# Attention scores of a hybrid encoder block: the keys' low part multiplied over 128 rows instead of 64

## The chip, the cores and the metric

The kernel runs as one program on one core of a Trainium2 chip. The metric is the device time of an execution in microseconds. It is given as the median of the runs; single executions are shown with the profile, which was taken from one further execution.

## The reference

The reference is one layer of a bidirectional encoder, 1024 tokens of width 1024, in float32. A mixer with two branches (a Hyena long convolution and grouped-query attention) is followed by an expert-choice feed-forward layer with 16 experts. The part that matters here is the attention: 8 query heads of width 64, and 2 heads of keys and values, each shared by 4 query heads.

```python
q = (apply_axial_rope(rms_norm(q, q_gain), cos, sin) * (HEAD_DIM ** -0.5))
k = apply_axial_rope(rms_norm(k, k_gain), cos, sin)
...
def block(qblk):                       # 128 queries
    s = jnp.einsum('bkgqd,bksd->bkgqs', qblk, k)
    p = jax.nn.softmax(s, axis=-1)
    return jnp.einsum('bkgqs,bksd->bkgqd', p, v)
```

## The kernel before

**Two parts of each number.** TensorE's operands are in a shortened 32-bit float type. To keep the precision, the kernel splits an operand into a high part and the low rest, and adds up several products of parts in one PSUM bank. The helper `mm3` (lines 141 to 144) does this with three matmuls: high by high, high by low, low by high.

**Stages.** `mixer_head` computes the Hyena branch, the projections and the layouts of queries, keys and values. `attention` computes the scores, the softmax and the product with V, and fills in Hyena's output projection (`hyena_out`). `merge` and `project` combine the branches and add the residual. `experts` runs the feed-forward layer, for which most of the weights are loaded.

**Layout of queries and keys.** A head has only 64 channels, and a matmul can contract over 128 rows (partitions). The queries of a head, `QT[h]`, therefore hold both parts in one tile of 128 rows: for an even head the low rows are the high part and the upper rows the low part, for an odd head it is the other way round (lines 609 to 619). The keys are held in `KT[0][kv]` (high part) and `KT[1][kv]` (low part), each with the same 64 channels written twice, to the lower and the upper rows (lines 600 to 604). So one matmul of 128 rows with `KT[0]` gives (high + low part of the queries) times the high part of the keys. The second matmul adds the low part of the keys. Its rows `pr` are those of the queries' high part alone: 0 to 63 for an even head, 64 to 127 for an odd one.

**The order of the work in attention.** A unit is a head and two blocks of 128 queries, so there are 32 units, and each has 4 steps of 256 keys: 128 steps. In each step the loop at lines 867 to 878 traces: the transposes of the exponentials (`turned`, line 790) with the split of the result into `ph` on ScalarE (line 794) and `pl` on VectorE (line 795); one quarter of a later unit's scores (`scores`, lines 773 and 774); in two of three steps, a piece of Hyena's output projection (line 849); and the product of the previous step with V (`values`, lines 808 and 809). The scores run six quarters ahead of the steps. After two quarters, a block of queries has all its scores, and VectorE takes the maxima of the rows (line 779), ScalarE the exponentials (line 781). After the last step of every second unit `finish` scales the result (lines 814 to 827). The framework's scheduler fixes the order on each engine at build time, following this trace.

**Buffers.** The scores have two PSUM tiles of two banks (`pS`), the transposed exponentials two banks (`pM`), the results and the Hyena projection two (`pT`); `ph` and `pl` have two buffers each, the exponentials six. `QT` has two buffers, so the next head's queries are loaded while a head is worked on; the keys of the second head are loaded when the third query head starts. These loads are issued by GpSimd (lines 737 and 747), and those of the weights by SyncE.

**What follows attention.** The first weights of the experts are loaded when a certain step of the projection is done (line 963, kept as `late`).

Of the kernel before, what the change touches and what calls it, by code (L numbers as in the profile page):

```python
# [17 lines left out]
DRAM = bass.MemoryType.DRAM  # L18
# [33 lines left out]
def block(tc, xT, cols_d, rows_d, mlp_d, w4_d, dfc_d, idf_d, rope_d, wada_d, win_d, why_d, watt_d, wout_d, wr_d,  # L52
# [3 lines left out]
    mm = nc.tensor.matmul  # L56
# [44 lines left out]
    @contextmanager  # L101
    def lane(n):
        """work for the gaps of what is traced outside: a later place in the scheduler's order"""
        keep = tc.cur_priority
        tc.cur_priority = max(lanes.get(n, 0), 1000000 * n)
        yield
        lanes[n] = tc.cur_priority
        tc.cur_priority = keep

    @contextmanager  # L110
    def in_order():
        """each engine runs what is traced inside in the order of the trace"""
        traced = nc.cur_bb.bb.instructions
        first = len(traced)
        yield
        prev = {}
        for i in traced[first:]:
            if i.engine in (mybir.EngineType.PE, mybir.EngineType.Activation, mybir.EngineType.DVE):
                if i.engine in prev:
                    tc.add_manual_dep(i, prev[i.engine], mybir.DependencyInfo(  # L120
                        mybir.DependencyClass.NoSync, mybir.DependencyReason.DATA), reason="in_order")
                prev[i.engine] = i.name

    def wait(late, early):
        """holds an instruction back for its turn"""
        tc.add_manual_dep(late.ins, early.ins.name, mybir.DependencyInfo(
            mybir.DependencyClass.Sync, mybir.DependencyReason.DATA), reason="wait")
# [18 lines left out]
    def rsqrt(r, v, t):  # L146
        """r = v ** -0.5, the square root's table refined by a Newton step"""
        nc.scalar.activation(r, v, AF.Sqrt)
        nc.vector.reciprocal(r, r)
        nc.vector.tensor_mul(t, r, r)  # L150
        nc.vector.tensor_mul(t, t, v)
        nc.vector.tensor_scalar(t, t, -0.5, 1.5, op0=ALU.mult, op1=ALU.add)
        nc.vector.tensor_mul(r, r, t)

    def adaln(acc, w, k):
        """one step in k of silu(c) @ w_ada, by partitions"""
        if k == 0:
            nc.vector.tensor_scalar(acc, w, siluc[:, 0:1], None, op0=ALU.mult)
        else:
            nc.vector.scalar_tensor_tensor(acc, w, siluc[:, k:k + 1], acc, op0=ALU.mult, op1=ALU.add)  # L160
# [19 lines left out]
    def mixer_head():  # L180
# [16 lines left out]

        # ---- Hyena filters' hidden layers, x's norms, the first shift and scale, h^T
        mlp = f4([128, NMLP])
# [38 lines left out]
        def columns(row):  # L238
            """a row of 1024 as the columns of [128, 8]"""
            t = z4([1, 1024])  # L240
            for hf in range(2):
                nc.scalar.copy(t[:, hf * 512:hf * 512 + 512], row[hf])
            ps = pM([128, 8])
            for m in range(8):
                mm(ps[:, m:m + 1], t[:, m * 128:(m + 1) * 128], ones[0:1, 0:1], start=True, stop=True)
            return ps
# [124 lines left out]

        # ---- input projection
        def win_block(m, evac, n=0):
# [25 lines left out]

        # ---- long convolutions  # L400
        def split2(t):
# [119 lines left out]
        spectra(1)  # L521
        # ---- q, k and v: norms, rotary positions, layouts for the products
        for m in range(12, 18):
# [81 lines left out]
        for i in range(2):  # L605
            for h in range(2):
                nc.sync.dma_start(KT_s[i, h], K[i][h].bitcast(F32))
        # the upper rows are those of the even heads' high parts and of the odd heads' low parts
        for b_ in range(4):
# [97 lines left out]

        # ---- the branch gates, and between them the rest of adaLN's projection
        after, tc.cur_priority = tc.cur_priority, before
# [14 lines left out]
    def attention(right):  # L724
# [29 lines left out]
        def scores(u, Ps):  # L754
            """in four steps: the scores of two blocks of queries, the rows' maxima, the exponentials"""
            h, i = u
            kv = h // 4
            if i == 1 and h < 7:
                QTs[h + 1], load = query(h + 1)
                wait(load, exps[-1])  # L760
            if u == (2, 0):
                keys(1)
            QT = QTs[h]
            pr = slice(h % 2 * 64, h % 2 * 64 + 64)
            if i % 2 == 0:
                rss[h, i // 2] = w("rs", [128, 12], bufs=3)
            rs = rss[h, i // 2]
            for j in range(2):
                qs = slice((i * 2 + j) * 128, (i * 2 + j + 1) * 128)
                S = pS()  # L770
                for n in range(2):
                    ns = slice(n * 512, n * 512 + 512)
                    mm(S[:, n], QT[:, qs], KT[0][kv][:, ns], start=True, stop=False)
                    mm(S[:, n], QT[pr, qs], KT[1][kv][pr, ns], start=False, stop=True)
                    if n == 0:
                        yield
                Sf = S.rearrange("p n k -> p (n k)")
                c = (i % 2) * 2 + j
                nc.vector.tensor_reduce(rs[:, c:c + 1], Sf, axis=AX.X, op=ALU.max, negate=True)
                P = w("P", [128, 1024], bufs=6)  # L780
                exps.append(nc.scalar.activation(P, Sf, AF.Exp, bias=rs[:, c:c + 1], accum_out=rs[:, 4 + c:5 + c]))
                Ps.append(P)
                yield

        def turned(u, kk, Ps):
            """P^T's next two blocks of keys, split"""
            ps = pM()
            for n in range(2):
                for j in range(2):
                    nc.tensor.transpose(ps[:, n * 256 + j * 128:n * 256 + j * 128 + 128],  # L790
                                        Ps[j][:, (kk * 2 + n) * 128:(kk * 2 + n + 1) * 128], ident)
            ph = w("ph", [128, 512], F32R)
            pl = w("pl", [128, 512], F32R)
            nc.scalar.copy(ph, ps)  # L794
            nc.vector.tensor_sub(pl, ps, ph)  # L795
            return u, kk, ph, pl
# [31 lines left out]

        # ---- Hyena's output projection and gate, between the heads
        yh = yp.tile([128, 4, 1024], F32R, name="yh")  # L830
# [87 lines left out]
    def project(mTh, mTl, rc):  # L918
        """x1 = x + gt1 * (merged @ w_out), by columns d; its rows to DRAM; logits and sums of squares"""
        es = ExitStack()  # L920
# [22 lines left out]
        for m in range(8):  # L943
# [48 lines left out]
            for k in (0, 1) if m == 0 else (m + 1,) if m < 7 else ():  # L992
                adaln(acc, wload(wada_d[3, k]), k)
        # logits = r * (x1 @ (G2 w_router)) + sh2 @ w_router
        lT = wk.tile([NE, 1024], F32, name="lT", tag="sq", bufs=2)
# [27 lines left out]
    def choose(aff, r, rc, pT, w):  # L1023
        """the slot of each token in each expert's 128 (or -1), tokens in order; w and r as bf16 parts;
        the last instruction of TensorE before the choice"""
        es = ExitStack()
# [5 lines left out]

        # experts on partitions, in four chunks of tokens: each chunk's largest 128 in order
        ps = pT([128, 2, 128])
# [6 lines left out]
        for i in range(16):  # L1041
            V.max(m8[:, i], cur)
            nc.scalar.copy(up[0:64, 15 - i], m8[64:128, i])
            if i < 15:
                V.match_replace(wb[i % 2], m8[:, i], cur, -1.0)
                cur = wb[i % 2]
        # bf16 parts of the weights and of r, exact together
        wa = rc.tile([128, 8, NE, 3], BF16, name="wa")
# [11 lines left out]
        nc.gpsimd.tensor_copy(ra[:, :, 1], slots[:, 0:8])  # L1060
        # the largest 128 of two lists: of one's i-th and the other's i-th from the end, the larger;
        # the result falls, then rises; it is sorted, one of two chunks with its sign turned
        ab = [w("hl", [128, 512])[0:64, 0:128] for i in range(2)]
# [3 lines left out]
        a, b = ab  # L1067
# [9 lines left out]
        V.tensor_reduce(T, b[0:32], axis=AX.X, op=ALU.min)  # L1077
        # the 128th largest, to each token's partition; those above it, and of those equal to it the first
        Tb = pT([128, NE])
# [27 lines left out]
    def experts(aff, r, rc, raws, n_raw, late):  # L1107
# [16 lines left out]
        def load(src, n):  # L1124
            """1 MB in n rows a partition; not before the projection's end, nor ahead of the first tokens' gather"""
            raw = raws.tile([128, 4, 512], F32, name="raw", tag="raw", bufs=n_raw)
# [21 lines left out]
        def halves(src, e):  # L1148
            cuts = 4 if e == NE - 1 else 1
            o = []  # L1150
            for i in range(2):
                raw = load(src[:, None, i * 2048:i * 2048 + 2048], 1)
                h = w("eh", [128, 4, 512], F32R, 5)
                l = w("el", [128, 4, 512], F32R, 5)
                # the first of them while VectorE chooses
                eng = nc.gpsimd if len(loaded) <= 9 else nc.vector
# [115 lines left out]
        for e in range(NE):  # L1272
            for f in range(4):
# [4 lines left out]
                last = (e, f)  # L1278
                # the next expert's tokens, each step behind work that covers the wait for it
                if e + 1 < NE:  # L1280
# [160 lines left out]
```

## Time and profile before

The median of three runs is 2301.83 us (2300.32 to 2301.86). The profiled execution has a span of 2299.0 us from the first to the last instruction.

| from the profile | value |
|---|---|
| runs, median | 2301.83 us |
| profiled execution, span | 2299.0 us |
| TensorE matmuls, busy | 2188.9 us, 95% |
| TensorE weight loads, busy | 1687.6 us, 73% |
| VectorE, busy | 1909.1 us, 83% |
| ScalarE, busy | 1307.3 us, 57% |
| mean granted TensorE clock | 0.981 |
| DMA, mean rate over the span | 256 GB/s |

A busy share is the time with an instruction at work on the engine, divided by the span; matmuls are pipelined, so that one starts while the one ahead is still counted. PE stands for TensorE's matmuls, PEld for its weight loads, DVE for VectorE, ACT for ScalarE, POOL for GpSimd, SP for SyncE. In a group such as `pS<-KT,QT 64*128 64x512`, the result stands ahead of the arrow, then the operands; `64*128` is the rows and columns of the array that are used, and `64x512` the moving operand, rows by columns.

### The profile page before, as it was taken

To read this page: it belongs to the slowest core of one execution; us is meant where nothing else is said; L and a number is where in the kernel's file an instruction comes from. 1 tells how busy PE (TensorE), PEld (TensorE's weight loads), DVE (VectorE), ACT (ScalarE), POOL (GpSimd) and SP (SyncE) were. 2 spreads that over 40 slices of the span, in tenths; PEclk is the share of its full clock that TensorE was granted. 3 is DMA by queue.
4 is the path that set the end of the run, shared out by engine and by line. 5 is a ranking of instruction groups with operands and counts; after the bars stand their busy time and mean duration, and the time that the engine had idled before them with its cause. 6 is when DMAs were issued, how large, how long until landed. Compare 5 with 4: busy or idle time off the path is not lost. (4 is left out here: it accounts for less than half of the span.)

```text
span 2299.0 us, 26847 instructions
## 1 busy us (share of the span) xinstructions
PE 2188.9 (95%) x10076; PEld 1687.6 (73%) x10076; DVE 1909.1 (83%) x2149; ACT 1307.3 (57%) x1424; POOL 126.2 (5%) x130
## 2 busy tenths in 40 slices
PE   5799999999999999999699999999999999999997
PEld 1487887878677777766477777777777777777776
DVE  6888897998887777743798998988989889898886
ACT  5554454242376555212477676767677676776775
POOL 1011000010000000000400010000000000000000
PEclk8899999999999999999799999999999999999999
DMA  7155755554532112756599999999999999999994
GB/s 276 29 146 195 282 201 162 176 166 138 165 119 79 55 62 70 247 196 248 207 360 361 365 343 360 351 365 373 353 373 369 363 374 353 369 371 364 371 336 152
DMA packets 138134, 588.87 MB, mean 256 GB/s; under 512 B 13714, under 2 KB 34450, under 8 KB 88724
## 3 DMA queue, kind: packets, MB, share of 16 engines
q1 hardware_dynamic: 122308, 546.25, 63.5%
q0 software_dynamic: 15696, 40.90, 6.9%
q8 instruction: 79, 1.29, 0.2%
q14 instruction: 51, 0.42, 0.1%
HBM read 530.48 MB, written 56.62 MB: 255 GB/s over the span
## 5 line engine op out<-in xcount | busy, mean ns | idle before, releaser
L1161 DVE TENSOR_TENSOR el<-raw,eh 128x2048 fp32r<-128x2048 f32 (+1 forms) x451 | 861.5, 1946 | 66.6 <-ACT eh L1160 66.4
L1160 ACT CAST eh<-raw 128x2048 fp32r<-128x2048 f32 (+1 forms) x456 | 719.0, 1635 | 62.0 <-PE py L144 31.6
L142 PE MATMUL pM<-eh,xh 128*128 128x512 f32 x1024 | 406.9, 397 | 8.1 <-ACT eh L1160 6.3
L143 PE MATMUL pM<-el,xh 128*128 128x512 f32 x1024 | 406.4, 397 | 8.5 <-DVE el L1161 8.3
L144 PE MATMUL pM<-eh,xl 128*128 128x512 f32 x1024 | 402.1, 393 | 0.0
L143 PEld LDWEIGHTS pM<-el,xh 128*128 128x128 f32 x1024 | 192.9, 188 | 61.8 <-DVE el L1161 25.1
L142 PEld LDWEIGHTS pM<-eh,xh 128*128 128x128 f32 x1024 | 192.7, 188 | 50.7 <-ACT eh L1160 9.1
L142 PE MATMUL pM<-hT,wh 128*128 128x512 f32 x544 | 217.6, 400 | 4.7 <-ACT wh L137 3.7
L144 PEld LDWEIGHTS pM<-eh,xl 128*128 128x128 f32 x1024 | 192.9, 188 | 37.7
L144 PE MATMUL pM<-hT,wl 128*128 128x512 f32 x544 | 216.2, 398 | 0.6 <-DVE wl L138 0.6
L143 PE MATMUL pM<-hT,wh 128*128 128x512 f32 x544 | 216.5, 398 | 0.0
L143 PE MATMUL py<-el,hh 128*128 128x512 f32 x512 | 207.1, 404 | 1.3 <-DVE el L1161 1.3
L142 PE MATMUL py<-eh,hh 128*128 128x512 f32 x512 | 203.7, 398 | 1.9 <-ACT hh L1236 1.9
L144 PE MATMUL py<-eh,hl 128*128 128x512 f32 x512 | 202.3, 395 | 0.1
L137 ACT CAST wh<-wr 128x1024 fp32r<-128x1024 f32 (+1 forms) x60 | 56.0, 934 | 166.7 <-PE pM L143 82.4
L142 PEld LDWEIGHTS pM<-hT,wh 128*128 128x128 f32 x544 | 102.8, 189 | 29.1 <-ACT wh L137 4.2
L794 ACT CAST ph<-pM 128x512 fp32r<-128x512 f32 x128 | 74.9, 585 | 84.6 <-PE pM L790 79.4
L144 PEld LDWEIGHTS pM<-hT,wl 128*128 128x128 f32 x544 | 102.6, 189 | 25.0 <-DVE wl L138 1.3
L143 PEld LDWEIGHTS pM<-hT,wh 128*128 128x128 f32 x544 | 102.8, 189 | 23.6
L142 PEld LDWEIGHTS py<-eh,hh 128*128 128x128 f32 x512 | 96.1, 188 | 28.5 <-ACT hh L1236 6.3
L795 DVE TENSOR_TENSOR pl<-pM,ph 128x512 fp32r<-128x512 f32 x128 | 87.2, 687 | 34.2 <-ACT ph L794 33.6
L143 PEld LDWEIGHTS py<-el,hh 128*128 128x128 f32 x512 | 96.2, 188 | 24.6 <-DVE el L1161 3.1
(367 smaller groups left out, 3468.6 us busy)
## 6 DMA issues: line engine op xcount, KB each, us to landing
raw<-in_wg_dram SPq DMA_DIRECT2D x128, 1024.0 KB, 7.1
raw<-in_wu_dram SPq DMA_DIRECT2D x128, 1024.0 KB, 7.1
raw<-in_wd_dram SPq DMA_DIRECT2D x128, 1024.0 KB, 7.8
wr<-in_win_dram SPq DMA_DIRECT2D x34, 512.0 KB, 3.6
dc<-in_dfc_dram POOLq DMA_DIRECT2D x48, 256.0 KB, 3.0
wr<-in_wada_dram SPq DMA_DIRECT2D x24, 512.0 KB, 3.7
st<-in_wada_dram SPq DMA_DIRECT2D x16, 512.0 KB, 10.2
H<-H_s SPq DMA_DIRECT2D x16, 512.0 KB, 4.2
```

The lines of the kernel that those rows point to most:

```text
L137: nc.scalar.copy(h, raw)
L142: mm(o, a[0], b[0], start=start, stop=False)
L143: mm(o, a[0], b[1], start=False, stop=False)
L144: mm(o, a[1], b[0], start=False, stop=stop)
L794: nc.scalar.copy(ph, ps)
L795: nc.vector.tensor_sub(pl, ps, ph)
L1160: nc.scalar.copy(h[:, ks], raw[:, ks])
L1161: eng.tensor_sub(l[:, ks], raw[:, ks], h[:, ks])
```

## The change

The second product of the scores runs over all 128 rows of the queries and of the low part of the keys, and no longer over the 64 rows `pr`. The result gains the product of the queries' low part with the keys' low part. The lines of the helper variable are gone; comments are blanked elsewhere in the file, which is not shown.

```diff
             QT = QTs[h]
-            pr = slice(h % 2 * 64, h % 2 * 64 + 64)
             if i % 2 == 0:
                 rss[h, i // 2] = w("rs", [128, 12], bufs=3)
...
                     mm(S[:, n], QT[:, qs], KT[0][kv][:, ns], start=True, stop=False)
-                    mm(S[:, n], QT[pr, qs], KT[1][kv][pr, ns], start=False, stop=True)
+                    mm(S[:, n], QT[:, qs], KT[1][kv][:, ns], start=False, stop=True)
```

## Prediction

> **What bounds the kernel now.** I read the page's busy shares first, then the windows of the stretch in which the changed instructions run, then the groups of that stretch, its waits, and last the instructions in order of time. The chain that ended last was of no use: it holds only the final DMA and some issue time.
>
> ```profile
> span 2299.0 us, 26847 instructions
> PE 2188.9 (95%) x10076; PEld 1687.6 (73%) x10076; DVE 1909.1 (83%) x2149; ACT 1307.3 (57%) x1424; POOL 126.2 (5%) x130
> ```
>
> TensorE is busy for 95% of the whole span, but a busy TensorE may still be waiting inside an instruction, so the stretch has to be looked at by itself. The second product of the scores runs there:
>
> ```profile
> L774 PE MATMUL pS<-KT,QT x128: 490/498/504, 624.4 to 896.4; 64*128 64x512 f32 x128
> ```
>
> It starts 128 times, first at 624.4 us and last at 896.4 us. The windows around that (busy us and instructions of each engine, granted clock, DMA share, GB/s):
>
> ```profile
> 600.00:634.00 34.00, 28.90 (x122) 20.38 (x120) 26.57 (x32) 17.22 (x24) 4.75 (x9) 0.95 0.65 210
> 634.00:910.00 276.00, 275.97 (x1532) 205.57 (x1531) 209.35 (x286) 169.34 (x298) 4.99 (x10) 1.00 0.23 76
> 910.00:1010.00 100.00, 96.36 (x413) 71.10 (x413) 69.94 (x96) 23.11 (x35) 0.92 (x2) 1.00 0.66 219
> 1060.00:2299.00 1239.00, 1181.51 (x5427) 933.33 (x5426) 1072.89 (x1031) 833.48 (x720) 75.62 (x41) 0.98 0.91 341
> ...
> 640.00:660.00 20.00, 20.00 (x110) 14.37 (x109) 16.77 (x24) 15.15 (x30) 0.00 (x0) 1.00 0.35 117
> 800.00:820.00 20.00, 20.00 (x116) 15.09 (x115) 13.81 (x19) 11.20 (x20) 0.53 (x1) 1.00 0.22 79
> ```
>
> From 634 to 910 us, the attention proper, TensorE has no gap at all (275.97 of 276 us), VectorE is busy 209.35 us (76%), ScalarE 169.34 us (61%), and DMA has little to do (0.23). So TensorE's own stream sets the pace there. The last two rows are the window of 20 us in which VectorE is fullest, and the emptiest, of the 13 between 640 and 900 us.
>
> What TensorE does in that stretch, and beside what (groups from 634 to 911 us: busy us, mean ns of one, idle time just before them):
>
> ```profile
> L774 PE MATMUL pS<-KT,QT 64*128 64x512 f32 x123 | 61.0, 496 | 0.0
> L773 PE MATMUL pS<-KT,QT 128*128 128x512 f32 x122 | 54.7, 448 | 0.0
> L849 PE MATMUL pT<-yl,wh 128*128 128x512 f32 x64 | 25.6, 400 | 0.0
> L774 PEld LDWEIGHTS pS<-KT,QT 64*128 64x128 f32 x123 | 22.5, 183 | 28.9 <-issue 28.2
> L849 PEld LDWEIGHTS pT<-yh,wl 128*128 128x128 f32 x64 | 12.0, 188 | 11.3 <-issue 11.2
> L808 PEld LDWEIGHTS pT<-ph,Vhl 128*128 128x128 f32 x256 | 48.4, 189 | 12.0 <-issue 7.8 <-ACT ph L794 0.7 <-DVE ot L821 0.3
> ```
>
> A matmul of 64 rows takes longer (496 ns) than one of 128 rows and the same 512 columns in the same stretch (400 ns). And the weight loads of line 774 stand idle 28.2 us for "issue": they wait for nothing that a semaphore tells of. Durations overlap, so what counts is the time from one start to the next. TensorE's instructions in order of time (start, duration):
>
> ```profile
> 842.77 0.39 PE L849 MATMUL pT<-yh,wh 128*128 128x512 f32 x1
> 843.00 0.39 PE L849 MATMUL pT<-yl,wh 128*128 128x512 f32 x1
> 843.23 0.28 PE L808 MATMUL pT<-ph,Vhl 128*128 128x256 f32 x1
> ...
> 845.32 0.50 PE L849 MATMUL pT<-yh,wl 128*128 128x512 f32 x1
> 845.66 0.39 PE L773 MATMUL pS<-KT,QT 128*128 128x512 f32 x1
> 845.98 0.50 PE L774 MATMUL pS<-KT,QT 64*128 64x512 f32 x1
> 846.41 0.39 PE L808 MATMUL pT<-ph,Vhl 128*128 128x256 f32 x1
> 846.64 0.28 PE L809 MATMUL pT<-pl,Vhl 128*128 128x256 f32 x1
> 846.76 0.28 PE L808 MATMUL pT<-ph,Vhl 128*128 128x256 f32 x1
> ```
>
> In an undisturbed run a matmul of 512 columns is followed by the next after 0.23 us (842.77, 843.00, 843.23), one of 256 columns after 0.12 us (846.64, 846.76). Around a line 774 it is otherwise: 0.32 us from the first product to it, 0.43 us from it to the next, and the matmul behind it, of 256 columns, holds the next back for 0.23 us (846.41 to 846.64). The weight loads of the same moments say why:
>
> ```profile
> 843.00 0.19 PEld L808 LDWEIGHTS pT<-ph,Vhl 128*128 128x128 f32 x1
> 843.23 0.19 PEld L809 LDWEIGHTS pT<-pl,Vhl 128*128 128x128 f32 x1
> ...
> 845.98 0.18 PEld L774 LDWEIGHTS pS<-KT,QT 64*128 64x128 f32 x1 [0.36 <-issue]
> 846.41 0.19 PEld L808 LDWEIGHTS pT<-ph,Vhl 128*128 128x128 f32 x1 [0.25 <-DVE pl L795]
> 846.52 0.19 PEld L809 LDWEIGHTS pT<-pl,Vhl 128*128 128x128 f32 x1
> ```
>
> Between instructions of 128 rows a weight load starts together with the matmul ahead of its own (the load for 843.23 at 843.00) and is hidden. At line 774 it starts only with its own matmul (845.98), and so does the next full load (846.41): going from 128 rows to 64 and back, TensorE empties twice.
>
> On the 0.25 us of the last but one row the view names VectorE; the same gap follows line 774 where it names only issue, so I take it for the same thing.
>
> [...]
>
> **The change, part by part.** Nothing is added: the 128 second products keep their count, their 512 columns and their place; no DMA, no wait and no buffer is touched, since both halves of the low keys are loaded already. What changes is the form, from 64 to 128 rows, with three effects on TensorE for each instance:
>
> - the first product goes back to 0.23 us from 0.32: 0.09 us;
> - the second goes from 0.43 to 0.23: 0.20 us;
> - the one behind loses its exposed load: 0.23 to 0.12 us, or 0.34 to 0.23 where it has 512 columns (845.32 to 845.66): 0.11 us.
>
> Together 0.40 us. The price of a full-row second product is read off line 849, whose three matmuls accumulate in one bank in the same form; no row here shows two full loads of the very same queries in a row, which I put at no extra cost, because the load is 0.19 us and the matmul ahead gives it 0.23. In the attention proper 123 instances (of 128) stand: 123 x 0.40 = 49.2 us, and 5 stand before 634 us, where TensorE is busy 28.90 of 34 us and waits for others: between 0 and 2.0 us, taken as 0.
>
> Not all of it reaches the end. TensorE would then need 276 - 49.2 = 226.8 us, beside VectorE's 209.35 (92% of that). What is late next are the steps of P transposed: transposes on TensorE, the copy ph on ScalarE, the difference pl on VectorE, then the product with V. The waits from 634 to 911 us (total us, times, longest):
>
> ```profile
> ACT ph L794 <- PE pM L790: 79.4, 91, 2.6
> DVE pl L795 <- ACT ph L794: 33.6, 53, 1.3
> DVE rs L779 <- PE pS L774: 17.8, 22, 1.7
> DVE ot L821 <- ACT ot L820: 9.9, 10, 1.5
> DVE oT L827 <- ACT oT L825: 1.8, 3, 0.8
> PEld pT L809 <- DVE pl L795: 1.0, 4, 0.3
> ```
>
> TensorE waits for VectorE hardly at all today (1.0 us for pl). Behind a late pl queue the row maxima of the next scores (1.2 us each on VectorE), and for those the exponentials. Both ends of the loss: at best no stall, a gain of 49.2 (51.2 with the five early ones). At worst VectorE's waits for ScalarE all stay as they are, 33.6 + 9.9 + 1.8 = 45.3 us, and VectorE sets the stage at 209.35 + 45.3 = 254.7 us, a gain of 21.3. I expect those waits to shrink, because ScalarE itself waits for TensorE's transposes (79.4 us), which come sooner. For how dense TensorE stays with VectorE nearly full, the nearest row is the experts' stage: 1181.51 of 1239 us, 95%, with VectorE at 87%. So 226.8 / 0.95 = 238.7 us, a gain of 276 - 238.7 = 37.3 us.
>
> The stages behind move up rigidly: the merge, the projection and the experts start on results of attention, and the first expert weights wait for a step of the projection (line 963), not for the clock. DMA, at 0.91 in the experts' stage, gets no more to do and no less time. The sum: 2299.0 - 37.3 = 2261.7 us of span. The runs' median is 2301.83, 2.8 us above this span, so 2264.5 us, given as 2264.
>
> **The rivals.** *VectorE takes over as the bound.* Gain 21.3 us, 2280.5 us. For it: in the window at 640 us VectorE is busy 16.77 of 20 us, while TensorE there would need 20 - 0.40 x 123 x 20/276 = 16.4 us. Against it: that is the fullest of 13 windows, the emptiest has 13.81.
>
> *Everything passes through.* Gain 51.2 us, 2250.6 us. For it: buffers of two between the engines, and the 1.0 us that TensorE waits for pl today. Against it: VectorE would have to run at 92% with an order made for another pace.
>
> *Nothing changes.* This is so if the low keys' weight load stays exposed at 128 rows as well, and the drain belongs to the change of product rather than to the row form. [...] It would give 2301.8 us. [...]
>
> *Slower, through the clock.* With TensorE faster than its suppliers, gaps of some us appear at the heads' ends, and the granted clock falls behind each. The stretch before 634 us shows it: idle for 3.0 us (first row below), it then ran at 0.42 us from start to start instead of 0.23 (623.11 to 623.54), and its window has a clock of 0.95.
>
> ```profile
> 620.38 0.50 PEld L773 LDWEIGHTS pS<-KT,QT 128*128 128x128 f32 x2 [3.00 <-issue]
> 623.11 0.61 PE L144 MATMUL pT<-Zh,dc 128*128 128x512 f32 x1
> 623.54 0.42 PE L142 MATMUL pT<-Zh,dc 128*128 128x512 f32 x1
> ```
>
> One such event costs 3.0 us and 5% of 34 us, 4.7 us together. It takes eight of them, one in each head, to eat 37.3 us; two in each head, 75 us, would end at 2264.5 + 75 = 2339.5 us. Against it: the longest wait of any of these chains today is 2.6 us, and it is ScalarE's.
>
> **How the numbers follow.** The forecast, a gain between the two bounds with some stalls, gets 0.62 and gives the predicted 2264 us; its own range is 2255 to 2276. VectorE as the bound gets 0.18, everything passing 0.13, nothing 0.04, slower 0.03. The range takes in the first three, 0.93 in all, from 2250 to 2281 us; less would cut off one of the two bounds. I widen the lower end by a microsecond and the upper by two for the spread of the runs (2300.32 to 2301.86). A change under 0.2%, 4.6 us, can't be told from none. Faster: 0.62 + 0.18 + 0.13 = 0.93; same 0.04; slower 0.03.
>
> **What would show it.** In the changed profile the second product has the form 128*128, a mean near 400 ns, and no "issue" before its weight loads; the idle "issue" in front of lines 849 and 808 is gone with it. From start to start there should be 0.23 us before and after it. The stretch from the first scores to the last P transposed shrinks from 276 to some 239 us, with VectorE's busy time unchanged at 209 us and new, short waits of TensorE for pl and ph. The windows behind keep their lengths. The prediction is wrong in size if VectorE's idle time does not shrink with TensorE's, wrong in kind if a weight load of the second product still starts only with its matmul, or if the instructions come in another order than before.

## The result and the profile after

The changed kernel takes 2261.11 us (median of four runs, 2256.31 to 2262.78) against 2301.61 us of the kernel before on the same chip: a ratio of 0.9826 with a 95% interval from 0.9813 to 0.9840. It is faster by 40.5 us; the prediction had said 2264 us. The profiled execution has a span of 2259.4 us, 39.6 us less than that of before, and itself took 2261.17 us.

Where the 39.6 us lie is seen with the span cut at three events: the first and the last start of a product with V by `pl`, and the first cast of the experts' weights. The windows from the first of them to the end of the span, first of the kernel before and then of the changed one (busy us and instructions of PE, PEld, DVE, ACT, POOL; clock; DMA share; GB/s):

```profile
637.30:910.00 272.70, 272.67 (x1517) 203.61 (x1517) 206.74 (x283) 167.96 (x296) 4.46 (x9) 1.00 0.23 75
910.00:1090.70 180.70, 172.72 (x745) 125.64 (x745) 97.50 (x141) 38.89 (x65) 2.21 (x6) 0.97 0.64 222
1090.70:2299.00 1208.30, 1155.15 (x5305) 913.56 (x5303) 1064.26 (x1008) 824.06 (x701) 74.34 (x37) 0.98 0.92 345
```

```profile
637.40:870.80 233.40, 232.06 (x1516) 202.41 (x1517) 203.26 (x283) 167.41 (x296) 4.46 (x9) 1.00 0.27 88
870.80:1052.60 181.80, 172.81 (x745) 125.30 (x744) 97.53 (x141) 38.77 (x65) 2.21 (x6) 0.97 0.63 221
1052.60:2259.40 1206.80, 1153.04 (x5305) 912.32 (x5303) 1064.32 (x1008) 824.01 (x701) 74.34 (x37) 0.99 0.92 345
```

The first product with V starts at the same moment (637.3 and 637.4 us). The stage between the products, which I call the V window below, falls from 272.7 to 233.4 us: 39.3 of the 39.6 us. The two later stretches move up and keep their lengths within 1.5 us. VectorE and ScalarE run the same instructions as before and are busy 3.5 and 0.6 us less. The order of the instructions is the same on every engine.

The groups of the changed kernel from 634 to 871 us (the second product is line 773 now, the first 772, the Hyena projection 848, the products with V 807 and 808):

```profile
L772 PE MATMUL pS<-KT,QT 128*128 128x512 f32 x124 | 54.8, 442 | 1.0 <-ACT P L780 1.0
L773 PE MATMUL pS<-KT,QT 128*128 128x512 f32 x124 | 50.2, 404 | 0.0
L773 PEld LDWEIGHTS pS<-KT,QT 128*128 128x128 f32 x123 | 23.5, 191 | 0.5
L848 PEld LDWEIGHTS pT<-yh,wl 128*128 128x128 f32 x64 | 12.1, 189 | 1.6
L807 PEld LDWEIGHTS pT<-ph,Vhl 128*128 128x128 f32 x256 | 48.3, 189 | 8.3 <-DVE ot L820 2.1 <-ACT ph L793 1.4
```

The second product has 128 rows and a mean of 404 ns instead of 496, and the 28.2 us of "issue" ahead of its weight loads are gone; so are the 11.2 and 7.8 us of "issue" ahead of the two other groups. TensorE's instructions in order of time, and the weight loads under them:

```profile
814.32 0.39 PE L773 MATMUL pS<-KT,QT 128*128 128x512 f32 x1
814.55 0.40 PE L848 MATMUL pT<-yh,wl 128*128 128x512 f32 x1
814.78 0.40 PE L772 MATMUL pS<-KT,QT 128*128 128x512 f32 x1
815.01 0.39 PE L773 MATMUL pS<-KT,QT 128*128 128x512 f32 x1
815.35 0.39 PE L807 MATMUL pT<-ph,Vhl 128*128 128x256 f32 x1
```

```profile
814.55 0.19 PEld L772 LDWEIGHTS pS<-KT,QT 128*128 128x128 f32 x1
814.78 0.19 PEld L773 LDWEIGHTS pS<-KT,QT 128*128 128x128 f32 x1
815.35 0.19 PEld L807 LDWEIGHTS pT<-ph,Vhl 128*128 128x128 f32 x1 [0.38 <-DVE ot L820]
```

Four starts in a row are 0.23 us apart, where it was 0.32 and 0.43 us around a second product. Directly behind a group of transposes, where 56 of the 120 first products of the V window stand, the distance was 0.41 us and is 0.32, so 0.09 us are saved there too. The second product's weight load (814.78) starts under the first product. The last rows show what has come in its place: the product with V now waits for VectorE (`ot`). The waits from 634 to 871 us (total us, times, longest):

```profile
ACT ph L793 <- PE pM L789: 43.4, 68, 1.6
DVE pl L794 <- ACT ph L793: 14.4, 29, 1.2
DVE ot L820 <- ACT ot L819: 6.2, 10, 1.3
PEld pT L808 <- DVE pl L794: 4.4, 13, 0.7
PEld pM L789 <- DVE pl L794: 2.2, 6, 0.6
DVE oT L826 <- ACT oT L824: 0.9, 2, 0.5
```

### The profile page after: what moved, and what is told of

It reads as the page before. It is cut to its first block, busy times and chain, and to the rows that moved or that the text cites. A ratio compares the mean times of both kernels' runs of the same rounds, so it can differ in the third digit from the quotient of the medians.

```text
span 2259.4 us, 26847 instructions
## 1 busy us (share of the span) xinstructions
PE 2144.2 (95%) x10076; PEld 1684.7 (75%) x10076; DVE 1905.5 (84%) x2149; ACT 1306.7 (58%) x1424; POOL 126.3 (6%) x130
## 5 line engine op out<-in xcount | busy, mean ns | idle before, releaser
L144 PEld LDWEIGHTS py<-eh,hl 128*128 128x128 f32 x512 | 96.3, 188 | 21.2 <-DVE hl L1236 0.4
L1235 ACT CAST hh<-pT 128x512 fp32r<-128x512 f32 x64 | 37.3, 583 | 116.0 <-PE pT L1232 116.0
```

Source lines behind the costliest of these rows:

```text
L144: mm(o, a[1], b[0], start=False, stop=stop)
L1235: nc.scalar.copy(hh, pt)
```

## The experiments

The theory to test was that each change of form, from 128 rows to 64 and back, costs TensorE 0.40 us, and that a part of the saving is lost because VectorE becomes nearly full. This price is called a drain below. In the trace of the kernel before it stands as two weight loads that start only with their own matmuls, each 0.07 us before the matmul ahead is counted as over (the load at 845.98 with that one over at 845.66 + 0.39 = 846.05, the load at 846.41 with 845.98 + 0.50 = 846.48). The first four kernels ran with the kernel before at 2300.91 us, the next four at 2300.55 us, the last four at 2299.45 us.

**64 rows again, but in pairs.** Both first products of a block of queries come ahead of both second ones, which have 64 rows as in the kernel before.

```diff
-                for n in range(2):
-                    ns = slice(n * 512, n * 512 + 512)
-                    mm(S[:, n], QT[:, qs], KT[0][kv][:, ns], start=True, stop=False)
-                    mm(S[:, n], QT[:, qs], KT[1][kv][:, ns], start=False, stop=True)
-                    if n == 0:
+                pr = slice(h % 2 * 64, h % 2 * 64 + 64)
+                for i_ in range(2):
+                    r = pr if i_ else slice(0, 128)
+                    for n in range(2):
+                        ns = slice(n * 512, n * 512 + 512)
+                        mm(S[:, n], QT[r, qs], KT[i_][kv][r, ns], start=i_ == 0, stop=i_ == 1)
+                    if i_ == 0:
                         yield
```

> Undoes the row form, but halves the number of changes of form: the second products have 64 rows again, and both of a block of queries run one after the other, behind both first products (64 pairs instead of 128 single ones). Theory (the price is the draining of TensorE at a change of form, 0.40 us each time in and out): 64 x 0.40 = 25.6 us less than in the kernel before, some 2276 to 2280 us, and the second of a pair starts 0.23 us after the first. [...]

Measured: 2280.7 us, ratio 0.9909 (0.9892 to 0.9925), 20.2 us less than before. That is 0.7 us above the theory's range, and 7.4 us below the 2288.1 us that a saving at the neighbours alone would have given, 64 x (0.09 + 0.11) = 12.8 us. The scheduler left 54 of the 64 pairs together and pulled the others apart, so 54 drains are spared, 51 of them in the V window: 51 x 0.40 = 20.4 us. The V window falls from 272.7 to 253.2 us, 19.5 us. A pair in the trace: TensorE first, with the pair as one row (x2), then the pair's second product by itself, then the loads:

```profile
826.27 0.73 PE L775 MATMUL pS<-KT,QT 64*128 64x512 f32 x2
826.93 0.38 PE L809 MATMUL pT<-ph,Vhl 128*128 128x256 f32 x1
827.16 0.28 PE L810 MATMUL pT<-pl,Vhl 128*128 128x256 f32 x1
```

```profile
826.61 0.39 PE L775 MATMUL pS<-KT,QT 64*128 64x512 f32 x1
```

```profile
826.27 0.29 PEld L775 LDWEIGHTS pS<-KT,QT 64*128 64x128 f32 x2 [0.17 <-issue]
826.93 0.19 PEld L809 LDWEIGHTS pT<-ph,Vhl 128*128 128x128 f32 x1 [0.37 <-issue]
```

Two products of 64 rows take 0.66 us up to the next instruction. This sum is the theory's (0.43 + 0.23) and not that of two lone ones (0.43 + 0.43 = 0.86): the second one adds what a full one costs. How the sum is divided the theory did not have right: the second product starts 0.34 us after the first, and the next instruction 0.32 us after that. Both loads are over within 0.29 us of the first start, and a lone 64-row matmul is counted for 0.50 us (496 ns in the mean before), so the second load ran under the first 64-row matmul. The 64-row form is not dear in itself; the change of form is: TensorE's loads stand idle for 0.17 and 0.37 us at the two ends of the pair, and the view shows no gap between its two loads, which are in the same 64 rows.

**The control: pairs with 128 rows.** The same order, with all rows in both products.

```diff
-                for n in range(2):
-                    ns = slice(n * 512, n * 512 + 512)
-                    mm(S[:, n], QT[:, qs], KT[0][kv][:, ns], start=True, stop=False)
-                    mm(S[:, n], QT[:, qs], KT[1][kv][:, ns], start=False, stop=True)
-                    if n == 0:
+                for i_ in range(2):
+                    for n in range(2):
+                        ns = slice(n * 512, n * 512 + 512)
+                        mm(S[:, n], QT[:, qs], KT[i_][kv][:, ns], start=i_ == 0, stop=i_ == 1)
+                    if i_ == 0:
                         yield
```

> Control for the run with 64-row pairs: the same pairing of first and second products, with 128 rows. Theory: the order by itself is worth nothing, 2261 us as the changed kernel, within 3 us. Rival: the pairing itself changes the stalls (later or earlier maxima); then this run moves away from 2261 us and the run with 64-row pairs has to be read against it.

Measured: 2258.57 us, ratio 0.9816 (0.9799 to 0.9832); V window 234.4 us against 233.4. The pairing by itself is worth nothing in this stage, and the interval holds the changed kernel's ratio.

**Half of the change.** 64 rows for the first 512 keys, 128 for the last.

```diff
+                pr = slice(h % 2 * 64, h % 2 * 64 + 64)
                 for n in range(2):
                     ns = slice(n * 512, n * 512 + 512)
+                    r = slice(0, 128) if n else pr
                     mm(S[:, n], QT[:, qs], KT[0][kv][:, ns], start=True, stop=False)
-                    mm(S[:, n], QT[:, qs], KT[1][kv][:, ns], start=False, stop=True)
+                    mm(S[:, n], QT[r, qs], KT[1][kv][r, ns], start=False, stop=True)
```

> Half of the change: the second product has 64 rows for the first 512 keys and 128 rows for the last 512. Theory (0.40 us for each 64-row product, and stalls of TensorE come only when VectorE gets nearly full): TensorE's need falls by 64 x 0.40 = 25.6 us while VectorE stays under 84% of the stage, so nearly all of it reaches the end: 2276 to 2278 us. Rival (each us saved loses the same fifth to the coupling with ScalarE and VectorE, as 51.2 became 40.5): 25.6 x 0.79 = 20.2 us, 2281 us.

Measured: 2278.31 us, 22.6 us less than before; V window 251.6 us, 21.1 us less. The runs went from 2275.06 to 2282.14 us, too far apart for the two expectations (2276 to 2278, and 2281), and the profiled execution was the fastest of them. The windows say that the first half brought 21.1 us and the second 18.2, for 60 x 0.40 = 24.0 us of TensorE's need in each: both lose something, the second more.

**The next bound: a shorter second product.** On the changed kernel, the second product covers 128 of each 512 keys; the low part of the other keys is left out.

```diff
-                    mm(S[:, n], QT[:, qs], KT[1][kv][:, ns], start=False, stop=True)
+                    mm(S[:, n, 0:128], QT[:, qs], KT[1][kv][:, n * 512:n * 512 + 128], start=False, stop=True)
```

> On the changed kernel: the second product covers only the first 128 of each 512 keys, so the low part of the other keys is left out. The instructions keep their order on every engine, TensorE is relieved of about 0.12 to 0.14 us x 128 = 15 to 18 us, VectorE of nothing. Theory (VectorE and the steps through ScalarE now limit the stage, 208 us of work in 239): at most a third comes through, 2255 us or more, and TensorE's waits for pl, ph and ot grow by ten us or so. Rival (TensorE's own stream is still the only limit): all of it comes through, 2243 to 2246 us.

Measured: 2254.42 us, ratio 0.9801 (0.9785 to 0.9818). The short product is counted for 0.22 us instead of 0.40 (medians of 222 and 396 ns). My estimate from start to start is 0.11 us instead of 0.23, the distance of the transposes, which have 128 columns too (0.109 us in the median in the changed kernel): 0.12 us x 128 = 15.4 us of relief, 14.4 of it in the V window. The V window falls from 233.4 to 229.5 us, 3.9 us, or a quarter. The waits of TensorE's weight loads for `pl` grow from 4.4 + 2.2 to 7.7 + 4.2 us:

```profile
PEld pT L808 <- DVE pl L794: 7.7, 23, 0.9
PEld pM L789 <- DVE pl L794: 4.2, 12, 0.9
```

So TensorE's own stream is no longer the only limit. Whether that is VectorE's load or the length of the chain behind it was the question for the rest.

**VectorE relieved.** The differences `oTl` and `yl` go to GpSimd.

```diff
-            nc.vector.tensor_sub(oTl[h // 2][a:a + 64, hs], t[a:a + 64], oTh[h // 2][a:a + 64, hs])
+            nc.gpsimd.tensor_sub(oTl[h // 2][a:a + 64, hs], t[a:a + 64], oTh[h // 2][a:a + 64, hs])
...
-                nc.vector.tensor_sub(yl[:, :, sl], t, yh[:, :, sl])
+                nc.gpsimd.tensor_sub(yl[:, :, sl], t, yh[:, :, sl])
```

> On the changed kernel: the 16 differences oTl and the 8 differences yl go from VectorE to GpSimd, 24 x 0.68 = 16.3 us of VectorE's 208 us in the stage; some instructions get another place in the order. Theory (the 12 us that TensorE now loses in the stage are VectorE's lateness): a third to a half of them goes, 2255 to 2257 us, and TensorE's waits for pl fall from 7 us in total to 3 or 4. Rival (the waits are the length of single chains, not VectorE's load): 2260 to 2262 us.

Measured: 2259.23 us, ratio 0.9816 (0.9802 to 0.9831), between the two expectations and nearer the rival's. The V window:

```profile
634.20:868.90 234.70, 231.57 (x1516) 202.12 (x1517) 190.82 (x260) 168.06 (x296) 34.05 (x31) 1.00 0.26 86
```

VectorE has 12.4 us less to do (190.82 against 203.26), and the window is no shorter. The waits of the weight loads for `pl` are 5.4 + 2.3 us, against 4.4 + 2.2. The theory that VectorE's load makes the stalls got nothing from this run; GpSimd, though, takes 1.28 us for one such difference where VectorE takes 0.68, and the order of the instructions moved, so it is not a clean refutation.

**VectorE burdened, after and before.** The same 24 differences are done twice.

```diff
-            nc.vector.tensor_sub(oTl[h // 2][a:a + 64, hs], t[a:a + 64], oTh[h // 2][a:a + 64, hs])
+            nc.vector.tensor_sub(oTl[h // 2][a:a + 64, hs], t[a:a + 64], oTh[h // 2][a:a + 64, hs]); nc.vector.tensor_sub(oTl[h // 2][a:a + 64, hs], t[a:a + 64], oTh[h // 2][a:a + 64, hs])
...
-                nc.vector.tensor_sub(yl[:, :, sl], t, yh[:, :, sl])
+                nc.vector.tensor_sub(yl[:, :, sl], t, yh[:, :, sl]); nc.vector.tensor_sub(yl[:, :, sl], t, yh[:, :, sl])
```

> On the changed kernel: the 24 differences oTl and yl are done twice, 16.3 us more work for VectorE in the stage, 224 us against TensorE's need of 227. Theory (VectorE is the second bound of the stage after the change): 8 to 12 us slower than the changed kernel, 2269 to 2273 us. Rival (VectorE's load does not matter): within 3 us of 2261 us.

> The same doubling of 24 differences on the kernel before; the order of the instructions changes as in its counterpart on the changed kernel. VectorE then has 226 us in a stage of 276. Both theories: within 4 us of the kernel before, 2300 to 2305 us; if it is slower by as much as its counterpart, the price is one of order or of the chains and not of VectorE's load.

Measured: 2269.82 us on the changed kernel, ratio 0.9859 (0.9843 to 0.9875), and 2308.30 us on the kernel before, ratio 1.0030 (1.0018 to 1.0042). The first is in the theory's range, the second some 3 us above what I had expected. The V windows grow by 10.7 and 8.3 us. The trace of the doubled kernel before shows one place, in the first head, where a score waits 4.5 us for the exponentials. The wait of the weight load, from 655 to 690 us:

```profile
PEld pS L773 <- ACT P L781: 4.5, 1, 4.5
```

The window of 20 us with that gap, with a clock of 0.83:

```profile
660.00:680.00 20.00, 15.71 (x78) 12.42 (x77) 16.74 (x25) 10.54 (x19) 0.53 (x1) 0.83 0.35 105
```

The doubled kernel after the change has a wait of 4.9 us there too, so that place has to be kept apart from the load. The two doubled kernels have the same order of instructions on every engine, as the two undoubled ones have, so the V window can be cut at the same instruction in all four: the first product with V by `pl` of the third head. The rows are the last six heads of the kernel before, the same doubled, the changed kernel, the same doubled, and last the run above with the differences on GpSimd:

```profile
705.60:910.00 204.40, 204.39 (x1140) 153.08 (x1139) 152.40 (x208) 121.75 (x214) 2.35 (x5) 1.00 0.18 57
718.80:924.30 205.50, 205.44 (x1141) 152.96 (x1140) 160.24 (x220) 122.16 (x214) 2.35 (x5) 1.00 0.17 55
696.00:870.80 174.80, 174.22 (x1139) 152.09 (x1139) 150.28 (x209) 121.74 (x214) 2.35 (x5) 1.00 0.21 70
701.80:880.40 178.60, 175.91 (x1140) 152.36 (x1140) 158.10 (x221) 122.24 (x214) 2.35 (x5) 1.00 0.21 67
694.80:868.90 174.10, 173.16 (x1139) 152.11 (x1139) 143.72 (x197) 122.23 (x214) 17.69 (x16) 1.00 0.21 68
```

In the first two heads the doubling costs 7.2 us before the change and 6.9 after, nearly the same. In the last six, VectorE has 7.8 us more to do in both kernels; the kernel before takes 1.1 us longer, the changed one 3.8. So more work for VectorE does hold the changed kernel up, by about half of what is added, and hardly the kernel before. Less work does not help as much: 6.6 us less for VectorE in these heads shortened them by 0.7. Each row is one execution, and that of the doubled kernel before was the slowest of its seven, 7.2 us above their median, so this is an indication rather than a proof.

**The product with V one step later.** The loop keeps two steps waiting instead of one, with three buffers for `ph` and `pl` and, for their space, two for `m1` in the merge.

```diff
-            ph = w("ph", [128, 512], F32R)
-            pl = w("pl", [128, 512], F32R)
+            ph = w("ph", [128, 512], F32R, 3)
+            pl = w("pl", [128, 512], F32R, 3)
...
-            if len(due) > 1:
+            if len(due) > 2:
...
-                m1 = wk.tile([128, 512], F32, name="m1", tag="m1", bufs=3)
+                m1 = wk.tile([128, 512], F32, name="m1", tag="m1", bufs=2)
```

> On the changed kernel: the product with V follows its transposes by two steps instead of one, with three buffers for ph and pl instead of two (and, for their space, two instead of three for m1 in the merge). VectorE's work stays the same. Rival (the length of the chain from transposes through ph and pl to the product costs the 12 us): the waits for ph, pl and ot before the product with V go, 2255 us or less. Theory (VectorE's load and the two banks of the transposes limit it): under 3 us gained, 2258 to 2262 us, the waits move to the transposes.

Measured: 2270.73 us, ratio 0.9865 (0.9849 to 0.9880), slower than the changed kernel by some 10 us; neither expectation held for the whole. The V window is short, 227.2 us with TensorE busy for 226.98, but it starts at 655.9 us: in the new order ScalarE has a copy of Hyena's result (`yh`) ahead of the first exponentials, waits for its transfer, and the scores wait 14.8 us. Its waits from 600 to 660 us:

```profile
PE pS L772 <- ACT P L780: 14.8, 1, 14.8
ACT yh L837 <- DMA yq<-y_s: 14.0, 2, 9.5
```

Part of the short window is work that had moved out of it; the next run takes the late start away. The profiled execution was the slowest of the four, 9.2 us above their median, so the others may have waited less.

**The same, in the same space.** Five buffers for the exponentials instead of six, `m1` as it was; the exponentials come ahead of `yh` again.

```diff
-                P = w("P", [128, 1024], bufs=6)
+                P = w("P", [128, 1024], bufs=5)
```

> On the changed kernel: the product with V follows its transposes by two steps, with three buffers for ph and pl, and five for the exponentials instead of six, so that the space stays the same and attention can start when it did before. Theory now (the length of the chain from the transposes through ph and pl to the product with V costs TensorE the 6.6 us above its need of 226.8 between the first and the last product with V): these 233.4 us become 227 to 229, as in the first run with later products (227.2), the start is not late any more, 2254 to 2257 us. Rival (what that run gained in the middle is the work that its late start had moved out of it, or VectorE's load limits): 232 us or more between the products, 2260 us or more.

> Control: the changed kernel with three buffers for ph and pl and five for the exponentials, and the product with V one step behind as before; the order of all instructions is that of the changed kernel. Theory (it is the lateness that helps, not the buffers): 2260 to 2262 us, 233 us between the first and the last product with V. Rival (the buffers alone free the chain): 2254 to 2257 us.

Measured: 2258.02 us with the later product, ratio 0.9817 (0.9802 to 0.9833), and 2259.58 us with the buffers alone, 0.9827 (0.9811 to 0.9843). The V windows are 229.8 and 234.5 us. With the later product the window is 4.7 us shorter than its control (3.6 than the changed kernel), between the two expectations, and the buffers alone gain nothing. In the runs only 1.6 us of it can be seen, and the intervals overlap. The lateness does take away waits: in the V window those of the loads for `pl`, `ot` and `ph` ahead of the products with V are down to 0.5 us. But the window also holds less: ten matmuls of TensorE fewer start in it, since four transposes now lie ahead of its first product with V and six matmuls of the merge behind its last. At 0.11 and 0.23 us from start to start that is some 1.8 us of work. By this estimate 1.8 to 2.9 us are left for the lateness, three to four tenths of the 6.6 us that I had put down to the chain.

**The same on the kernel before, and with the shorter product.** The two edits above, on the 64-row kernel; and together with the second product over 128 of each 512 keys, which leaves out the low part of the other keys.

> The same later product with V, on the kernel before (64 rows). Its TensorE stream needs 276 us in the attention proper, and its waits for pl, ph and ot are some 5 us in total. Theory (the waits for the chain are in the main a consequence of the faster stream): 0 to 4 us gained, 2297 to 2302 us. Rival (the later product is worth 6 us by itself, whatever the rows): 2294 to 2296 us.

> The later product with V, together with the second product over only 128 of each 512 keys (the low part of the other keys is left out). Without the later product that relief of 15.4 us of TensorE brought 4.7 us in the profile. Theory (the chain was what held it back): with it, at least two thirds of the 15.4 us come through against the run with later products alone, 217 us or less between the first and the last product with V, although VectorE then has 203 us of work in it. Rival (VectorE's load is the floor): less than half comes through, 221 us or more.

Measured: 2299.32 us on the kernel before, ratio 0.9998 (0.9988 to 1.0008), no gain, as expected: with 64 rows the later product has little to cover. Its V window is 270.3 us, 2.4 us less, of which 1.8 are again the ten matmuls. With the shorter product 2250.80 us, ratio 0.9785 (0.9770 to 0.9801), V window 224.1 us: 5.7 us less than with the later product alone, of 15.4. That is the rival's case. Even with a looser chain TensorE's relief comes through by little more than a third in the window, and by nearly half in the runs (7.2 us of 15.4).

```profile
637.00:866.80 229.80, 228.03 (x1509) 201.09 (x1508) 203.21 (x283) 166.50 (x296) 4.45 (x9) 1.00 0.25 86
```

```profile
637.70:861.80 224.10, 219.41 (x1510) 194.56 (x1509) 202.72 (x283) 166.21 (x296) 4.47 (x9) 0.99 0.26 88
```

The upper row is the later product alone, the lower one with the shorter second product. VectorE is busy 88% of the upper window and 90% of the lower one, and TensorE has gaps in the lower. That fits VectorE as the nearest bound below 230 us, and so does the price of the doubled differences after the change; but the run that relieved VectorE did not gain, so what holds the stage there stays open. A version that leaves no product out and is clearly faster than the changed kernel was not found: 2258.0 us with the later product lies within the intervals.

## Why the prediction was right

**The drain.** The terms 0.09, 0.20 and 0.11 us hold where the prediction had read them: after the change the three distances are 0.23 us, or 0.12 where a product with V stands behind. The pairs show the price without the change: 51 drains spared in the V window, 20.4 us expected, 19.5 found. The unknown price of two full loads of the same queries in a row, put at nothing, is nothing (814.55 and 814.78 above).

**The five early instances**, taken as 0 to the end: the first product with V started at 637.3 us before and 637.4 after. Their value was 0.

**The loss.** In the V window stand 120 instances, 48.0 us at 0.40 us each, which would leave TensorE a need of 272.7 - 48.0 = 224.7 us; it took 233.4, a loss of 8.7 us. The prediction had 11.9 (238.7 - 226.8), from the density of 95% in the experts' stage; by the same division it was 224.7 / 233.4 = 96%. So this term was 3.2 us too large. Three instances fewer stand in this window than in the prediction's stretch, which takes back 1.2 us, and the gain here is 39.3 us instead of 37.3. The remaining 1.2 us of the 3.2 between the runs' gain (40.5) and the forecast lie outside of the window and between the profiled execution and the medians.

That the borrowed 95% came so near was partly luck. Of the 57.5 us in which TensorE is idle in the experts' stage before the change, one single wait makes up 15.5, which is one event and not the density of a stage beside a nearly full VectorE (waits of the matmuls from 1060 us to the end):

```profile
PE pT L1080 <- DVE T L1077: 15.5, 1, 15.5
```

Nor are the 8.7 us all stalls. Since the order is the same, each matmul of the V window can be set beside its counterpart and the distances to the next start compared. They shrank by 12.5 us ahead of the second products, by 20.6 at them and by 9.5 behind them, 42.7 us in all and not 48.0; everywhere else they grew by 3.3 us. The 5.3 us missing at the three places are in part new waits, and in part a saving that was smaller: where transposes follow a second product, the third distance went from 0.17 us to 0.14 only. How they divide stays open.

**What is late next.** `pl` and `ot`, as said: TensorE's waits for `pl` rose from 1.0 us at line 809 to 4.4 at the same place. VectorE's waits for ScalarE, which would have made it the bound had they stayed at 45.3 us, fell to 14.4 + 6.2 + 0.9 = 21.5 us. As a reason for the loss I had named VectorE being nearly full. That is shown only in part: 7.8 us more of VectorE's work in the last six heads cost 3.8 us, and 1.1 before the change, but relieving it brought next to nothing, and making the product with V later took some of the waits away.

**The stages behind** moved up as forecast; their lengths changed by 1.1 and -1.5 us.

**The rivals.** VectorE as the sole bound (2280.5 us) and everything passing (2250.6 us) both lie outside the measured runs. "Nothing changes" fell with the loads of the second product that start under their predecessors (814.78 above, under the first product's 0.40 us). "Slower, through the clock" did not come: the clock stayed at 1.00 in the V window. But a low clock beside such a gap was seen: the 20 us around the wait of 4.5 us, in the doubled run on the kernel before, have a clock of 0.83, and in the kernel before the windows 620 to 622 and 622 to 624 us, behind the gap that the prediction shows, have 0.54 and 0.61, then 1.00.

## What to carry to other kernels

Read a matmul's price from start to start, with its neighbours: here half of the extra 0.40 us of each 64-row product stood at its neighbours, 0.09 us at the one ahead and 0.11 at the one behind. In this stream of full-row matmuls of 512 columns a lone half-row one costs 0.63 us to insert where a full-row one with useless but harmless rows costs 0.23; if the rows must be half, put such products together (a pair took 0.66 us up to the next instruction, two lone ones 2 x 0.43). And when the bounding engine is relieved until it comes near the next one, expect only a part of any further relief to come through: here, with TensorE's need within about a tenth of VectorE's work (225 and 203 us), the shorter product brought a quarter to a half of its relief.

## What the runs showed that was not expected

In the run with pairs, the second of two 64-row matmuls on the same rows has its weight load under the first, as the full ones have there: two loads within 0.29 us, and 0.30 for two full ones (824.00), with 0.66 us for the 64-row pair. And a change that only shifts buffers and adds a step of delay moved a copy on ScalarE ahead of the first exponentials, at a price of 14.8 us of waiting in the profiled execution; the order on each engine has to be looked at after such an edit.
